# Values of four heads in one pass with tokens on partitions, and decay-level matmuls placed inside later projections

## The chip, the cores and the metric

The kernel runs on one core of one Trainium2 chip. The metric is the device time of one execution in microseconds, the median of several runs. A profile is one execution recorded by the hardware; its times are used below to work out costs.

## The reference, cut to what matters

One inference step of one layer that has two groups of heads. 512 prompt tokens and 64 sample tokens (8 sequences of 8) go through one input projection of 2048 inputs. Its outputs feed eight heads of sparse attention (a, 128 wide each), an indexer that picks the keys, and four heads of gated linear attention (b, keys 128 wide, values 256 wide).

```python
z = jnp.einsum('btd,de->bte', h, w_in)
qa, ka, va, ga, qi, ki, wi, qb, kb, vb, gb, ab = jnp.split(z, offs, axis=-1)
...
# sparse attention: scores against the picked keys, softmax, then the values va
# gated linear attention, in chunks:
cum = jnp.cumsum(at, axis=2)                       # log decays, summed along the chunk
o_inter = jnp.einsum('bhtk,bhkv->bhtv', qt * jnp.exp(cum), S)
att = jnp.einsum('bhtk,bhsk,bhtsk->bhts', qt, kt, decay)
o = o_inter + jnp.einsum('bhts,bhsv->bhtv', att, vt)
S_new = jnp.exp(last) * S + jnp.einsum('bhsk,bhsv->bhkv', kt * jnp.exp(last - cum), vt)
...
return einsum('bte,ed->btd', concatenate([a, bpart]), w_out)
```

The values `va` (1024 columns) and `vb` (1024 columns) are the part of the projection that the change concerns. New keys and values are outputs as well.

## The kernel before, in words

**Projection.** The input is kept transposed in SBUF, 16 pieces of 128 inputs by 576 tokens, each split into a high and a low part (`xh`, `xl`). `gemm(b)` (L207 on) computes one block of 128 output columns for all 576 tokens, with the columns on partitions: four weight pieces come by DMA (`wload`, L178), ScalarE casts the high part (L181), VectorE or GpSimd takes the low part (L183), and TensorE does three products for each of 16 input pieces in two halves of 288 tokens. That is 96 matmuls at L219 for a block. There are 65 such blocks or narrower ones in a fixed sequence: first block, indexer, then q, k, v and g of attention heads 0 to 7, then q, k and two value blocks of each gated head 0 to 3, then eight gates and the out-projection (L1133 to L1138, 512 columns moved against 128 stationary tokens or inputs).

**Values before.** A value block comes out with columns on partitions, though the attention needs tokens there. So `head_v` (L594 on) and the loop of the gated head (L982 on) write it to SBUF and turn it with five TensorE transposes (L601 and L607, L988 and L991).

**Accumulators.** PSUM holds two accumulators of two banks for `gemm` (`pg`), three single banks (`pm`) that everything else shares in turn, and one bank for the paged attention.

**Work beside the projections.** Generators are advanced between the weight pieces: `fill` advances the scoring of cached index keys (`first`, rate `RF`) and later the paged attention of the sample tokens (`us`, rates `R0`, `R1`); `pump` advances the selection of the top keys (`bg`), which runs mostly on VectorE during attention heads 0 to 3.

**A gated head before.** `log_decay(h)` makes the summed log decays `cum`: two matmuls into `ps_z` (L850), then ScalarE takes an absolute value, an exponential and a logarithm (L851, L853, L854), VectorE adds and scans (L855, L857). Seven levels follow (block sizes 64 to 1): GpSimd subtracts (L887, L888, tile `lv_d`), ScalarE takes the exponential (L889), VectorE multiplies with keys and queries (L890, L891), and TensorE does a run of small matmuls into `pl` for the first four levels and another for the rest (`run`, L252 and L255). `kD` (L958 to L961) is the key factor for the state; it is turned by TensorE. The recurrence over the four chunks and the sample states comes after the value blocks. `log_decay(h+1)` is called ahead of the recurrence of head h, and `cum` has two buffers.

**What sets the order.** Each engine runs its own list of instructions in the order in which a scheduler has placed them. The scheduler goes by the order of the code and by buffers coming free; weight loads and the tails of runs are given a higher priority. Within a list, an instruction that waits holds all that stand behind it.

Of the kernel before, what the change touches and what calls it, by code (L numbers as in the profile page):

```python
# [119 lines left out]
def build(tc, I, O):  # L120
# [4 lines left out]
    R0, R1, RF = 0.42, 0.8, 2  # L125
# [187 lines left out]
    spill_a = [dp.tile([P, TP], F32, name=f"sa{h}") for h in range(HA)]  # L313
    spill_o = [dp.tile([P, T], F32, name=f"so{h}") for h in range(HA)]
# [35 lines left out]
    rs2 = v2(rstd)  # L350
    sst2 = pa.tile([P, 5], F32, name="sst2")
# [3 lines left out]
    def token_scales():  # L355
        sst = pr.tile([P, 5], F32, name="sst")
        ve.memset(sst, 1.0)
        for i in range(5):
            r = P if i < 4 else TS
            xt = pr.tile([P, D], F32, name="xt", bufs=2)  # L360
            with tc.issue_after(wloads[3]):
                sy.dma_start(xt[:r], I["xp"][P * i : P * (i + 1)] if i < 4 else I["xs"])
            se.activation(xt[:r], xt[:r], AF.Square, accum_out=sst[:r, i : i + 1])
# [3 lines left out]
        for j in range(2):  # L367
            pst = mm1("ps_st")
            for i in (range(4), (4,))[j]:
                n = (P, TS)[j]  # L370
                dg = pr.tile([P, P], F32, name="dg", bufs=2)
                ve.tensor_scalar(out=dg[:, :n], in0=ident[:, :n], scalar1=sst[:, i : i + 1], scalar2=None, op0=ALU.mult)
# [220 lines left out]

    def head_v(h):  # L594
        ps = gemm(11 + 4 * h)
        vT = ev.tile([P, T], F32, name="ev_v", tag="e1", bufs=2)
        ve.tensor_tensor(out=v2(vT), in0=ps, in1=rs2, op=ALU.mult)
        sy.dma_start(O["vT"][h], vT)
        pt = mm1("pt")
        for i in range(4):  # L600
            pe.transpose(pt[:, P * i : P * (i + 1)], vT[:, P * i : P * (i + 1)], ident)  # L601
        vh = px["p"].tile([P, 512], F32R, name="vh")
        vl = px["p"].tile([P, 512], F32R, name="vl")
        se.copy(vh, pt)
        ve.tensor_tensor(out=vl, in0=pt, in1=vh.bitcast(F32), op=ALU.subtract)
        pt = mm1("pt")
        pe.transpose(pt[:, :P], vT[:, T - P : T], ident)  # L607
        se.copy(vaS[TS:, P * h : P * (h + 1)], pt[TS:, :P])
# [52 lines left out]
    def head(h, bg, n):  # L661
        if h > 1:
# [4 lines left out]
        elif h == 1:  # L667
            q, k = qk1
        else:
            q = head_q(0)  # L670
            pump(bg, n)
            k = head_k(0)
            pump(bg, n)
            qk1.append(head_q(1))
            qk1.append(head_k(1))
# [5 lines left out]
        if h > 0:  # L681
            Pi = head_scores(h, q, k)
        v = head_v(h)
        pump(bg, n)
        if h == 0:
            Pi = head_scores(h, q, k)
        g1 = head_g(h)
        pump(bg, min(n, 3))
# [105 lines left out]
    head(0, bg, 17)  # L794
    head(1, bg, 3)
    head(2, bg, 3)
    head(3, bg, 3)
# [46 lines left out]
    def log_decay(h):  # L844
# [11 lines left out]
        cum = gl.tile([P, T], F32, name="cum", bufs=2)  # L856
# [3 lines left out]
    cum_next = log_decay(0)  # L860
    for h in range(HB):
        cum = cum_next
        b0 = 41 + 4 * h
        ps = gemm(b0)
        qT = gl.tile([P, T], F32, name="qT")
# [3 lines left out]
        ve.tensor_tensor(out=v2(kT), in0=ps, in1=rs2, op=ALU.mult)  # L869
        cP = cum[:, :TP].rearrange("p (i t) -> p i t", t=P)  # L870
        cS = cum[:, TP:T].rearrange("p (i t) -> p i t", t=DT)

# [5 lines left out]
        for B in (64, 32, 0, 16, 8, 4, 2, 1):  # L878
# [57 lines left out]
            if B in (16, 1):  # L936
                run(*(m for level in reversed(mms) for m in level))
# [6 lines left out]
        for w in range(2):  # L944
# [3 lines left out]
            )  # L948

        eC = ev.tile([P, T], F32, name="ev_ec", tag="e0", bufs=2)  # L950
        se.activation(eC, cum, AF.Exp, scale=G)
        eL = gl.tile([P, 12], F32, name="eL", bufs=2)
        po_.tensor_copy(eL[:, 0:4].unsqueeze(2), eC[:, :TP].rearrange("p (i t) -> p i t", t=P)[:, :, P - 1 : P])
        po_.tensor_copy(eL[:, 4:12].unsqueeze(2), eC[:, TP:T].rearrange("p (i t) -> p i t", t=DT)[:, :, DT - 1 : DT])
        qE = gl.tile([P, T], F32, name="qE", tag="lv_q")
        ve.tensor_mul(qE, qT, eC)
        kD = gl.tile([P, T], F32, name="kD", tag="lv_d", bufs=4)
        po_.tensor_tensor(out=kD[:, :TP].rearrange("p (i t) -> p i t", t=P), in0=cP[:, :, P - 1 : P].to_broadcast([P, 4, P]), in1=cP, op=ALU.subtract)  # L958
        po_.tensor_tensor(out=kD[:, TP:T].rearrange("p (i t) -> p i t", t=DT), in0=cS[:, :, DT - 1 : DT].to_broadcast([P, NB, DT]), in1=cS, op=ALU.subtract)
# [3 lines left out]
        for i in range(4):
            pe.transpose(pt[:, P * i : P * (i + 1)], kD[:, P * i : P * (i + 1)], ident)
        kDt = gl.tile([P, 4, P], F32, name="kDt")
        se.copy(kDt, pt.rearrange("p (i d) -> p i d", i=4))
        pt = mm1("pt")
        pe.transpose(pt[:, :P], kD[:, T - P : T], ident)
        kDs = ev.tile([TS, P], F32, name="kDs", tag="e1", bufs=2)
        se.copy(kDs, pt[TS:, :P])  # L970
        ks = [gl.tile([96, P], F32R, name=f"ks{w}") for w in range(2)]
        for w in range(2):
            r = slice(32 * w, 32 * w + 32)
            lo_r, hi_r = ((32, 0), (0, 32))[w]
            se.copy(ks[w][hi_r : hi_r + 32], kDs[r])
            se.copy(ks[w][64:96], kDs[r])
            ve.tensor_tensor(out=ks[w][lo_r : lo_r + 32], in0=kDs[r], in1=ks[w][r].bitcast(F32), op=ALU.subtract)
        Qd = bass.AP(tensor=Qb.tensor, offset=Qb.offset, ap=[Qb.ap[0], [64, 4], [32 + DT, 2], [1, DT]])
        po_.tensor_copy(Qd, qE[:, TP:T].rearrange("p (m e t) -> p m e t", e=2, t=DT))

        vtok = gl.tile([P, 4, DV], F32, name="vtok")
        for half in range(2):  # L982
            ps = gemm(b0 + 2 + half)
            vT = ev.tile([P, T], F32, name="ev_v", tag="e1", bufs=2)
            ve.tensor_tensor(out=v2(vT), in0=ps, in1=rs2, op=ALU.mult)
            pt = mm1("pt")
            for i in range(4):
                pe.transpose(pt[:, P * i : P * (i + 1)], vT[:, P * i : P * (i + 1)], ident)  # L988
            se.copy(vtok[:, :, P * half : P * (half + 1)], pt.rearrange("p (i d) -> p i d", i=4))
            pt = mm1("pt")  # L990
            pe.transpose(pt[:, :P], vT[:, T - P : T], ident)  # L991
            se.copy(vS[:TS, P * half : P * (half + 1)], pt[TS:, :P])
# [6 lines left out]

        if h + 1 < HB:  # L1000
# [63 lines left out]
    for _ in us:  # L1064
        pass
# [202 lines left out]
```

## Time and profile before

| | us |
|---|---|
| median of 3 runs | 1247.18 (1246.3 to 1252.36) |
| the profiled execution | 1248.29 |
| its span, first to last instruction | 1246.5 |
| TensorE busy (98% of the span) | 1225.0 |
| VectorE busy (52%) | 651.1 |
| ScalarE busy (45%) | 558.2 |
| GpSimd busy (22%) | 269.9 |
| mean granted TensorE clock, share of full speed | 0.996 |

The profiled execution lies 1.1 us above the median of the runs and 1.8 us above its own span. A busy time adds up the recorded durations of an engine's instructions. Matmuls overlap in the records (one of 288 columns is recorded with some 300 ns, and the next starts sooner than that), so a price for TensorE is read from the distance of starts. The four gated heads take the stretch from 623 to 920 us, the gates come next, and the out-projection is last.

### The profile page before, as it was taken

The page shows a single profiled execution, that of the slowest core. Times are in us where ns is not written, and L with a number is a line of the kernel's source. Part 1 is how long each engine was busy: PE and PEld are TensorE (multiplying, and loading weights), DVE is VectorE, ACT ScalarE, POOL GpSimd, SP SyncE. Part 2 cuts the span into 40 slices and gives each one's busy share as a digit, 9 for nine tenths or more (in the row PEclk, how much of TensorE's full clock was granted, in tenths as well). Part 3 has the DMA queues.
Part 4 walks back from the last instruction along what each step waited for, and adds up shares of the span by engine and source line. Part 5 has one row for each costly group of instructions (what it writes and reads, how often), then busy time and mean ns, then how long its engine had stood idle before and what let it go on. Part 6 is the DMA issues. An engine that isn't in the chain of part 4 may idle for free.

```text
span 1246.5 us, 24845 instructions
## 1 busy us (share of the span) xinstructions
PE 1225.0 (98%) x9419; PEld 1119.2 (90%) x9419; DVE 651.1 (52%) x1330; ACT 558.2 (45%) x1072; POOL 269.9 (22%) x355
## 2 busy tenths in 40 slices
PE   9999999999999999999999999999999999999997
PEld 8899989999998979898988888888989998888896
DVE  6678899997543434342445444554445442323242
ACT  7966675353343423342344533635445432223233
POOL 0224663454511010100104121131120200102021
PEclk9999999999999999999999999999999999999998
DMA  9652233223726575664667576581414534334335
GB/s 314 219 157 88 70 95 95 87 83 99 254 90 241 193 243 181 219 209 161 229 201 238 191 264 209 202 264 60 152 62 155 179 99 136 102 101 123 89 113 171
DMA packets 117610, 200.58 MB, mean 161 GB/s; under 512 B 13922, under 2 KB 30579, under 8 KB 116787
## 3 DMA queue, kind: packets, MB, share of 16 engines
q1 hardware_dynamic: 116402, 197.55, 48.4%
q8 instruction: 74, 1.21, 0.4%
q10 hardware_dynamic: 1088, 1.45, 0.3%
q14 instruction: 46, 0.37, 0.1%
HBM read 180.06 MB, written 18.76 MB: 160 GB/s over the span
## 4 chain that ended last, share of the span: by engine, by line
PE 85%; DVE 5%; issue 4%; DMA 2%; ACT 2%; POOL 1%; SPq 1%; DVEq 0%; ACTq 0%; POOLq 0%
PE ps_g L219 50%; PE ps_g L227 6%; PE acc L1133 5%; PE acc L1135 5%; PE acc L1134 5%; PE pOs L255 2%; PE pS L255 1%; DVE wk L496 1%; PE acc L1137 1%; PE acc L1138 1%; PE pOs L252 1%; PE pS L252 1%; DVE top L493 1%; PE pt L649 1%; SPq L157 1%
## 5 line engine op out<-in xcount | busy, mean ns | idle before, releaser
L219 PE MATMUL ps_g<-xh,w_hi 128*128 128x288 f32 x1824 | 401.8, 299 | 1.1 <-ACT w_hi L198 0.6
L219 PE MATMUL ps_g<-xh,w_lo 128*128 128x288 f32 x1824 | 399.0, 298 | 0.0
L219 PE MATMUL ps_g<-xl,w_hi 128*128 128x288 f32 x1824 | 398.1, 297 | 0.0
L181 ACT CAST w_hi<-w_raw 128x512 fp32r<-128x512 f32 x316 | 194.8, 619 | 413.6 <-PE ps_g L219 237.2
L183 DVE TENSOR_TENSOR w_lo<-w_raw,w_hi 128x512 fp32r<-128x512 f32 x252 | 177.5, 708 | 305.3 <-ACT w_hi L181 301.9
L219 PEld LDWEIGHTS ps_g<-xh,w_hi 128*128 128x128 f32 x1824 | 295.7, 189 | 15.9 <-issue 11.7
L219 PEld LDWEIGHTS ps_g<-xh,w_lo 128*128 128x128 f32 x1824 | 295.9, 189 | 3.6 <-issue 2.1
L219 PEld LDWEIGHTS ps_g<-xl,w_hi 128*128 128x128 f32 x1824 | 296.3, 189 | 2.6 <-issue 1.3
L1134 PE MATMUL acc<-w_lo,mh 128*128 128x512 f32 (+1 forms) x320 | 110.7, 346 | 0.0
L1135 PE MATMUL acc<-w_hi,ml 128*128 128x512 f32 (+1 forms) x320 | 110.6, 346 | 0.0
L1133 PE MATMUL acc<-w_hi,mh 128*128 128x512 f32 (+1 forms) x320 | 110.3, 346 | 0.0
L183 POOL TENSOR_TENSOR w_lo<-w_raw,w_hi 128x512 fp32r<-128x512 f32 x64 | 87.4, 1367 | 74.4 <-ACT w_hi L181 60.2
L1153 POOL TENSOR_TENSOR y<-y,nfb 128x512 f32<-128x512 f32 (+3 forms) x25 | 27.7, 1123 | 190.3 <-ACT yjk L1152 190.3
L1134 PEld LDWEIGHTS acc<-w_lo,mh 128*128 128x128 f32 x320 | 60.5, 189 | 7.5
L1133 PEld LDWEIGHTS acc<-w_hi,mh 128*128 128x128 f32 x320 | 60.4, 189 | 7.5
L1135 PEld LDWEIGHTS acc<-w_hi,ml 128*128 128x128 f32 x320 | 60.4, 189 | 7.5
L887 POOL TENSOR_TENSOR lv_d<-cum 128x256 f32<-128x256 f32 (+1 forms) x28 | 20.8, 742 | 132.0 <-DVE cum L857 78.8
L571 POOL TENSOR_TENSOR ev_sw<-ev_sw,c_s 128x576 f32<-128x576 f32 x16 | 22.9, 1432 | 118.7 <-ACT ev_sw L568 118.5
L227 PE MATMUL ps_g<-xh,w_hi 128*128 128x448 f32 x128 | 47.2, 370 | 0.7 <-ACT w_hi L181 0.4
L227 PE MATMUL ps_g<-xh,w_lo 128*128 128x448 f32 x128 | 47.0, 368 | 0.3 <-DVE w_lo L183 0.3
L227 PE MATMUL ps_g<-xl,w_hi 128*128 128x448 f32 x128 | 47.0, 367 | 0.0
L421 DVE SCALAR_TENSOR_TENSOR sc<-rl,wtok,sc 128x256 f32<-128x256 f32 (+2 forms) x45 | 35.9, 831 | 4.3 <-ACT rl L416 4.0
(334 smaller groups left out, 1631.5 us busy)
## 6 DMA issues: line engine op xcount, KB each, us to landing
w_raw<-in_w SPq DMA_DIRECT2D x252, 256.0 KB, 3.1
kt<-in_ck SPq DMA_DIRECT2D x128, 256.0 KB, 5.2
vt<-in_cv SPq DMA_DIRECT2D x128, 256.0 KB, 5.2
w_raw<-in_wo SPq DMA_DIRECT2D x64, 256.0 KB, 2.8
xr<-in_xT SPq DMA_DIRECT2D x16, 288.0 KB, 4.6
xt<-in_xp SPq DMA_DIRECT2D x4, 1024.0 KB, 7.3
st<-in_state SPq DMA_DIRECT2D x8, 512.0 KB, 5.7
out_ss<-st SPq DMA_DIRECT2D x8, 512.0 KB, 3.8
```

The lines of the kernel that those rows point to most:

```text
L181: se.copy(hi, raw)
L183: lo_eng[0].tensor_tensor(out=lo, in0=raw, in1=hi.bitcast(F32), op=ALU.subtract)
L219: pe.matmul(ps[:, j, :HT], wt, xt[:, j * HT : (j + 1) * HT], start=(k == 0 and n == 0), stop=(k == NK - 1 and n == 2),)
L227: pe.matmul(ps[:, 0, :TQ], wt[:, c], xt[:, P:T], start=(k == 0 and n == 0), stop=(k == NK - 1 and n == 2))
L252: lead = first()
L255: f()
L421: ve.scalar_tensor_tensor(out=sc[i], in0=rl[:, :n], scalar=wcol, in1=sc[i], op0=ALU.mult, op1=ALU.add)
L571: po_.tensor_tensor(out=sw, in0=sw, in1=S128, op=ALU.mult)
L1133: pe.matmul(acc, mh[k][:, tsl], wh, start=(k == 0), stop=False)
L1134: pe.matmul(acc, mh[k][:, tsl], wl, start=False, stop=False)
L1135: pe.matmul(acc, ml[k][:, tsl], wh, start=False, stop=(k == NK - 1))
L1153: po_.tensor_tensor(out=yc, in0=yc, in1=nfb[:r, cs], op=ALU.mult)
```

## The change

Four things change.

1. The 16 value blocks become four calls of `vgroup(g)`, each for 512 value columns. Tokens are the stationary operand, 128 at a time, and 512 weight columns move. The 64 sample tokens sit beside their own low parts in one 128-wide tile `xs`, which GpSimd copies for each input piece. Four accumulators are the halves of two `pg` tiles; the fifth, `ps_v`, is a `pm` bank. ScalarE evacuates with the token scale, and the rows go to a DRAM tile `spill_v` (and to the output). `head_v` reads its 128 columns back, `recur` reads 256. The transposes of values go. Group 0 comes after the keys of attention head 1, group 1 in head 4, groups 2 and 3 in gated heads 0 and 1.
2. The gated head is cut into `project` (with `log_decay` at its start), `decays` (a generator that yields ahead of each run) and `recur`. The runs of `decays(h)` are called inside the projection that follows: in `vgroup` for heads 0 and 1, in the projections of head 3 for head 2, and in the first two gates for head 3.
3. `log_decay(h+1)` is called after `recur(h)`, `cum` has one buffer, and `kD` is made ahead of the levels.
4. Rates: `R1` 0.8 to 0.65, `RF` 2 to 1.1, and `pump` advances 10 and 4 steps in place of 17 and 3.

The diff, cut to its core:

```diff
+    def vgroup(g, step):
+        two = [pg.tile([P, 2, 512], F32, name="ps_g", tag="ps_g") for _ in range(2)]
+        accs = [two[0][:, 0], two[0][:, 1], two[1][:, 0], two[1][:, 1], mm1("ps_v")]
+        def mms(i, k):
+            wh, wl = w[k]
+            a, b = k == 0, k == NK - 1
+            if i == 4:
+                pe.matmul(accs[4], xs2[k], wh, start=a, stop=False)
+                pe.matmul(accs[4], xs2[k], wl, start=False, stop=b)
+            else:
+                c = slice(P * i, P * i + P)
+                pe.matmul(accs[i], xh[k][:, c], wh, start=a, stop=False)
+                pe.matmul(accs[i], xh[k][:, c], wl, start=False, stop=False)
+                pe.matmul(accs[i], xl[k][:, c], wh, start=False, stop=b)
+        w, xs2 = [], []
+        for k in range(NK):
+            w.append(wload(I["wv"][g, :, k : k + 1, :]))
+            xs = ev.tile([P, P], F32R, name="xs", tag="xs", bufs=4)
...
+            if k == 1:
+                for i in (0, 1, 4, 2, 3):
+                    for kk in (0, 1):
+                        mms(i, kk)
...
+            if k % 2:
+                fill()
+            if k % 4 == 3:
+                step(k // 4)
+        for i in range(4):
+            vt = ev.tile([P, 512], F32, name="v_tok", tag="e1", bufs=2)
+            se.activation(vt, accs[i], AF.Copy, scale=sst[:, i : i + 1])
+            sy.dma_start(spill_v[g][r], vt)
...
     def head_v(h):
-        ps = gemm(11 + 4 * h)
...
+        v32 = px["p"].tile([P, 4, P], F32, name="v32")
+        sy.dma_start(v32, spill_v[h // 4][:TP, P * (h % 4) : P * (h % 4) + P].rearrange("(i p) c -> p i c", p=P))
...
-        cum = gl.tile([P, T], F32, name="cum", bufs=2)
+        cum = gl.tile([P, T], F32, name="cum")
...
+    def project(h):
+        cum = log_decay(h) if h < 3 else None
...
+    def decays(h, qT, kT, cum):
+        cum = cum or log_decay(h)
...
             if B in (16, 1):
+                yield
                 run(*(m for level in reversed(mms) for m in level))
...
+    def recur(h, eL, qE, kDt, ks):
         vtok = gl.tile([P, 4, DV], F32, name="vtok")
-        for half in range(2):
-            ps = gemm(b0 + 2 + half)
...
+        sv = spill_v[2 + h // 2][:, DV * (h % 2) : DV * (h % 2) + DV]
+        sy.dma_start(vtok, sv[:TP].rearrange("(i p) c -> p i c", p=P))
...
-        if h + 1 < HB:
-            cum_next = log_decay(h + 1)
...
+    for h in range(HB):
+        if h < 3:
+            pj = project(h)
+            next(pj)
+            d = decays(h, *next(pj))
+        else:
+            d = decays(h, *qk3)
+        next(d)
+        if h < 2:
+            vgroup(2 + h, lambda q4: next(d) if q4 in (0, 2) else None)
+        elif h == 2:
+            pj = project(3)
+            next(pj)
+            next(d)
+            qk3 = next(pj)
+            next(d)
...
+        else:
+            mg, mg_s = pool("mixg", 1, side="right")
+            for i in range(2):
+                gate(i)
+                next(d)
+        recur(h, *kept[h])
```

TensorE's list before, where `log_decay(1)` stands: in the second value block of gated head 0. Names: `ev_v` is the value block being turned, `ps_z` the decay input, `ps_g` the projection that goes on.

```order
L252 MATMUL pOs<-vt,prT 32x512
L255 MATMUL pOs<-vt,prT 32x512 x7
L988 MATMUL pt<-c_ident,ev_v 128x128 x4
L991 MATMUL pt<-c_ident,ev_v 128x128
L850 MATMUL ps_z<-abS,wgS 128x288
L219 MATMUL ps_g<-xl,w_hi 128x288
```

The decay input of head 1 stands ahead of that head's own projections, which follow it with their 96 matmuls a block.

TensorE's list after, where `log_decay(1)` stands now: inside group 3, behind the last steps of `recur(0)` (`osb`, the output rows of head 0). The lines are those of the changed kernel: L896 is `ps_z`, L949 and L953 turn `kD`, L604 and L605 are the fifth accumulator of the group, `ob` and `pS` belong to the paged attention.

```order
L1110 MATMUL pt<-c_ident,osb 128x128 x4
L1113 MATMUL pt<-c_ident,osb 128x128
L896 MATMUL ps_z<-abS,wgS 128x288 x2
L823 MATMUL pt<-c_ident,ob 128x128 x4
L755 LDWEIGHTS selw
L755 MATMUL pS<-biasS,selw 128x512
L949 MATMUL pt<-c_ident,kD 128x128 x4
L953 MATMUL pt<-c_ident,kD 128x128
L604 MATMUL ps_v<-w_hi,xs 128x512
L605 MATMUL ps_v<-w_lo,xs 128x512
```

Between the decay input and the turning of `kD`, which is computed from it, four transposes and one matmul are left.

GpSimd's list before, for gated head 1. `lv_d` is a level's difference, `eL` and `Qb` small copies, `qz` a buffer of the paged attention.

```order
L887 TENSOR_TENSOR lv_d<-cum 128x288
L888 TENSOR_TENSOR lv_d<-cum 128x288
L953 COPY eL<-ev_ec 128x4
L954 COPY eL<-ev_ec 128x8
L979 COPY Qb<-qE 128x4x2x8
L698 MEMSET qz 128x512
L703 COPY qz<-qaS 128x4x8 x4
L958 TENSOR_TENSOR kD<-cum 128x512
L959 TENSOR_TENSOR kD<-cum 128x64
L961 TENSOR_TENSOR kD<-kT,kD 128x576
```

GpSimd's list after, for the same head.

```order
L944 TENSOR_TENSOR kD<-cum 128x64
L981 TENSOR_TENSOR lv_d<-cum 128x4x64
L982 TENSOR_TENSOR lv_d<-cum 128x4x64
L981 TENSOR_TENSOR lv_d<-cum 128x8x32
L982 TENSOR_TENSOR lv_d<-cum 128x8x32
L981 TENSOR_TENSOR lv_d<-cum 128x16x16
L982 TENSOR_TENSOR lv_d<-cum 128x16x16
L744 MEMSET qz 128x512
L938 COPY eL<-ev_ec 128x4
L939 COPY eL<-ev_ec 128x8
L965 COPY Qb<-qE 128x4x2x8
L946 TENSOR_TENSOR kD<-kT,kD 128x576
```

`kD` has moved from behind all levels to the front, but its last step, the multiplication with the keys, stands behind six differences of three levels and the small copies.

## Rows read from the trace of the kernel before

**Rows 1.** The page's busy times: us, share of the span, instructions.
```profile
PE 1225.0 (98%) x9419; PEld 1119.2 (90%) x9419; DVE 651.1 (52%) x1330; ACT 558.2 (45%) x1072; POOL 269.9 (22%) x355
```
**Rows 2.** TensorE's waits: us in total, times, longest us.
```profile
PE pl L252 <- DVE lv_d L891: 4.6, 2, 2.7
PE pq L466 <- ACT kcl L463: 1.6, 1, 1.6
...
PE pl L252 <- DVE lv_d L890: 1.4, 1, 1.4
```
**Rows 3.** TensorE's timeline, a gate block: start, us, then instructions and their count.
```profile
984.73 0.42 PE L219 MATMUL ps_g<-xh,w_hi 128*128 128x288 f32 x2
...
993.53 0.43 PE L219 MATMUL ps_g<-xh,w_hi 128*128 128x288 f32 x2
```
**Rows 4.** TensorE's timeline in the out-projection.
```profile
1120.01 0.39 PE L1133 MATMUL acc<-w_hi,mh 128*128 128x512 f32 x1
...
1121.37 0.39 PE L1133 MATMUL acc<-w_hi,mh 128*128 128x512 f32 x1
```
**Rows 5.** TensorE's timeline, the transposes of a value block of attention.
```profile
258.85 0.60 PE L601 MATMUL pt<-c_ident,ev_v 128*128 128x128 f32 x4
259.28 0.27 PE L607 MATMUL pt<-c_ident,ev_v 128*128 128x128 f32 x1
260.03 0.53 PE L219 MATMUL ps_g<-xh,w_hi 128*128 128x288 f32 x2 [0.48 <-DVE ga L614]
```
**Rows 6.** TensorE's timeline around the longest wait of a decay run.
```profile
908.08 0.18 PE L252 MATMUL pl<-lv_d 128*32 128x16 f32 x1 [2.69 <-DVE lv_d L891]
...
909.61 0.61 PE L219 MATMUL ps_g<-xh,w_hi 128*128 128x288 f32 x1
...
912.41 0.45 PE L219 MATMUL ps_g<-xh,w_hi 128*128 128x288 f32 x2
```
**Rows 7.** ScalarE's timeline, the log decay of gated head 0.
```profile
646.25 0.89 ACT L851 ACTIVATE ld_e<-ps_z,bgate 128x288 f32<-128x288 f32 x2 [1.24 <-PE ps_z L850]
647.16 1.28 ACT L853 ACT_TABLE_LOAD   x1
648.46 0.68 ACT L853 ACTIVATE ld_e<-ld_e 128x576 f32<-128x576 f32 x1
...
649.67 1.28 ACT L854 ACT_TABLE_LOAD   x1
650.96 0.69 ACT L854 ACTIVATE ld_e<-ld_e 128x576 f32<-128x576 f32 x1
```
**Rows 8.** VectorE's timeline, the same stretch.
```profile
652.54 1.36 DVE L857 TENSOR_TENSOR_SCAN cum<-reset,ld_m 128x576 f32<-128x576 bf16 x1
```
**Rows 9.** GpSimd's timeline, the first four levels of the same head.
```profile
654.05 0.62 POOL L887 TENSOR_TENSOR lv_d<-cum 128x256 f32<-128x256 f32 x1 [18.05 <-DVE cum L857]
...
655.20 1.15 POOL L887 TENSOR_TENSOR lv_d<-cum 128x256 f32<-128x256 f32 x1
...
659.50 0.61 POOL L888 TENSOR_TENSOR lv_d<-cum 128x256 f32<-128x256 f32 x1
660.06 0.38 POOL L953 COPY eL<-ev_ec 128x4 f32<-128x4 f32 x1
...
660.52 0.23 POOL L979 COPY Qb<-qE 128x64 f32<-128x64 f32 x1
```
**Rows 10.** GpSimd's groups by line: busy us, mean ns, idle before.
```profile
L1095 POOL TENSOR_TENSOR og<-og,mo 128x576 f32<-128x576 f32 x7 | 10.0, 1430 | 97.5 <-DMA ma<-sa 51.6 <-ACT og L1092 45.3 <-DMA mo<-so 0.6
...
L961 POOL TENSOR_TENSOR kD<-kT,kD 128x576 f32<-128x576 f32 x4 | 5.7, 1421 | 3.2 <-ACT kD L960 3.2
...
L958 POOL TENSOR_TENSOR kD<-cum 128x512 f32<-128x512 f32 x4 | 4.4, 1107 | 15.9 <-PE pl L255 15.9
...
L959 POOL TENSOR_TENSOR kD<-cum 128x64 f32<-128x64 f32 x4 | 1.6, 404 | 0.0
```
**Rows 11.** Busy time by stretch: from:to, width, then PE, PEld, DVE, ACT, POOL.
```profile
150.00:260.00 110.00, 106.54 (x785) 99.52 (x783) 105.58 (x248) 56.53 (x99) 54.89 (x62) 1.00 0.31 95
```

More of the change, by code (lines that the diff above doesn't have):

```diff
@@ L313, in build @@
     spill_a = [dp.tile([P, TP], F32, name=f"sa{h}") for h in range(HA)]
+    spill_v = [dp.tile([T, 512], F32, name=f"sv{g}") for g in range(4)]
     spill_o = [dp.tile([P, T], F32, name=f"so{h}") for h in range(HA)]
@@ L661, in head @@
     def head(h, bg, n):
[L662 removed]
+        if h == 1:
+            q, k = qk1
+        else:
             q = head_q(h)
@@ L666, in head @@
             pump(bg, n)
[L667 to L675, printed above, removed]
+        if h == 0:
+            for f in (head_q, head_k):
+                qk1.append(f(1))
+                pump(bg, n)
+            vgroup(0, lambda q4: pump(bg, 2))
             filler[0] = None
@@ L793, in build @@
     lo_eng[0] = po_
[L794 to L797, printed above, removed]
+    head(0, bg, 10)
+    head(1, bg, 4)
+    head(2, bg, 4)
+    head(3, bg, 4)
     lo_eng[0] = ve
@@ L855, in log_decay, with gate @@
         ve.tensor_tensor(out=mn, in0=mn, in1=e_, op=ALU.subtract)
-        cum = gl.tile([P, T], F32, name="cum", bufs=2)
+        cum = gl.tile([P, T], F32, name="cum")
         ve.tensor_tensor_scan(out=cum, data0=reset, data1=mn, initial=0.0, op0=ALU.mult, op1=ALU.add)
         return cum
-    cum_next = log_decay(0)
-    for h in range(HB):
-        cum = cum_next
+    og, kept = [], {}
+    def gate(i):
+        ps = gemm(57 + i)
+        g1 = mg.tile([P, T], F32, name=f"og{i}")
+        ve.tensor_tensor(out=v2(g1), in0=ps, in1=rs2, op=ALU.mult)
+        se.activation(g1, g1, AF.Silu)
+        o_t = ev.tile([P, T], F32, name="mo", tag="e0", bufs=2)
+        sy.dma_start(o_t, spill_o[i])
+        (po_ if i < 7 else ve).tensor_tensor(out=g1, in0=g1, in1=o_t, op=ALU.mult)
+        og.append(g1)
+    def project(h):
+        cum = log_decay(h) if h < 3 else None
         b0 = 41 + 4 * h
         ps = gemm(b0)
-        qT = gl.tile([P, T], F32, name="qT")
+        qT = gl.tile([P, T], F32, name="qT", bufs=2)
         ve.scalar_tensor_tensor(out=v2(qT), in0=ps, scalar=float(P ** -0.5), in1=rs2, op0=ALU.mult, op1=ALU.mult)
+        yield
         ps = gemm(b0 + 1)
@@ L963, in build @@
[L963 to L977, printed above, removed]
@@ L978, in build @@
-        Qd = bass.AP(tensor=Qb.tensor, offset=Qb.offset, ap=[Qb.ap[0], [64, 4], [32 + DT, 2], [1, DT]])
-        po_.tensor_copy(Qd, qE[:, TP:T].rearrange("p (m e t) -> p m e t", e=2, t=DT))
-        vtok = gl.tile([P, 4, DV], F32, name="vtok")
-        for half in range(2):
-            ps = gemm(b0 + 2 + half)
[L984 to L992, printed above, removed]
+        yield
@@ L1063, in build, with mixed @@
             sy.dma_start(spill_o[2 * h + half], o_t)
-    for _ in us:
-        pass
-    un_s.close()
+    for h in range(HB):
[14 more added lines that the diff above has]
+            next(d)
+            for _ in us:
+                pass
+            filler[0] = None
+            un_s.close()
+        else:
+            mg, mg_s = pool("mixg", 1, side="right")
[3 more added lines that the diff above has]
+        recur(h, *kept[h])
     gl_s.close()
-    mg, mg_s = pool("mixg", 1, side="right")
     mp, mp_s = pool("ms", 1)
     mh, ml, ms = [], [], []
-    def mixed(k, src, smp, pl, tags):
-        h = pl.tile([P, tags[2]], F32R, name="mh", tag=tags[0])
+    def mixed(k, src, smp, h, l):
         se.copy(h[:, :TP], src[:, :TP])
-        l = pl.tile([P, tags[2]], F32R, name="ml", tag=tags[1])
         ve.tensor_tensor(out=l[:, :TP], in0=src[:, :TP], in1=h[:, :TP].bitcast(F32), op=ALU.subtract)
@@ L1085, in mixed @@
         ms.append(s)
[L1087 removed]
     for i in range(8):
[L1089 to L1096 removed]
+        if i > 1:
+            gate(i)
         src = ev.tile([P, TP], F32, name="ma", tag="e1", bufs=2)
         sy.dma_start(src, spill_a[i])
[L1099 removed]
+        h, l = mp.tile([P, TP], F32R, name=f"mh{i}"), mp.tile([P, TP], F32R, name=f"ml{i}")
+        mixed(i, src, mixS[:, i, :], h, l)
     for i in range(8):
[L1101 removed]
+        h, l = xp.tile([P, T], F32R, name="mh", tag="xh"), xp.tile([P, T], F32R, name="ml", tag="xl")
+        mixed(8 + i, og[i], og[i][:, TP:T], h, l)
     banks = [0, None]
```

125 lines of the change are left out of this document (74 added, 51 removed).

## The prediction

> **What bounds the kernel now.** I read the page's busy times first: TensorE is recorded busy for 1225.0 of 1246.5 us, no other engine for more than 52% [rows 1]. The reader is to see a kernel whose time is the length of TensorE's list, plus its few waits. The second view is TensorE's waits: the largest are two kinds of wait of a decay run for VectorE's last multiplication of a level, 4.6 and 1.4 us, and one of 1.6 us for a cast of cached index keys [rows 2]. The third is the timeline, for the distance of starts. In a gate block the rows from 984.73 to 993.53 lie 66 matmuls apart: 8.80 / 66 = 0.1333 us for 288 columns [rows 3]. In the out-projection six matmuls of 512 columns take 1121.37 - 1120.01 = 1.36, or 0.2267 us each [rows 4]. Four transposes of a value block take 259.28 - 258.85 = 0.43, or 0.108 each [rows 5]. So two things decide: how many columns go through TensorE, and whether a new place appears where it has to wait.
>
> **The change, part by part.** Everything is summed against the profiled execution (1248.3 us); the median of the runs shown is 1.1 lower.
>
> *Values.* Sixteen blocks of 96 matmuls go: 1536 x 0.1333 = 204.8 us. Sixteen times five transposes go: 80 x 0.108 = 8.6 us. Each group needs 16 input pieces x (4 token tiles x 3 + 2 for the samples) = 224 matmuls of 512 columns, four groups 896: at 0.2267 that is 203.1 us. Their form (128 rows, 128 stationary columns, 512 moved) is that of rows 4, so I take that distance. The net is 203.1 - 204.8 - 8.6 = -10.3. A wait of 0.48 behind one block's transposes [rows 5] goes as well: **-10.8**. The value pass as such therefore saves little; it is the transposes that go. Bounds: -10.3, if that wait only moves, and -12, if the other blocks lose 0.1 each where TensorE changes from one form to another.
>
> *Waits of the decay runs.* The 4.6 + 1.4 = 6.0 us [rows 2] go, since a run now stands behind a stretch of 512-column matmuls. After the longest of them the projection runs at half its speed: 11 matmuls from 909.61 to 912.41 take 2.80 us [rows 6], against 11 x 0.1333 = 1.47; the clock was at its lower level, 1.2 GHz, after TensorE had stood still for 2.69 us. That is 1.3 more. Together **-7.3**.
>
> *Rates.* The index scoring is spread over a longer stretch, so its 1.6 us wait [rows 2] may go or stay. I take **-1.0**, between 0 and -1.6.
>
> *The new wait in gated head 1.* In the new list `log_decay(1)` stands behind the whole of `recur(0)`, inside value group 3, and the turning of `kD` follows with four transposes and one matmul of 512 columns between: 4 x 0.108 + 0.23 = 0.7 us of work [rows 4, 5]. `kD` depends on it. The chain, priced by head 0 in the trace: from the first absolute value at 646.25 through a table load of 1.28, an exponential of 0.68, another load of 1.28, a logarithm of 0.69 [rows 7] to the end of the scan, 652.54 + 1.36 = 653.90 [rows 8], is 7.65 us. Then GpSimd, in the order of its new list: the two subtractions of `kD`, 1.107 + 0.404 = 1.5 [rows 10]; six differences of three levels, of which eight took 660.11 - 654.05 = 6.06, so 6 x 0.76 = 4.5 [rows 9]; the small copies, 660.06 to 660.75, 0.7 [rows 9]; the multiplication, 1.4 [rows 10]. That is 8.1, in all 15.8, with 0.3 for the matmul itself 16.1 us. Less 0.7 of work: TensorE stands still for about **15.4**. Before, the same chain lay beside a head's own q and k blocks (2 x 96 x 0.1333 = 25.6 us) and cost nothing. Nothing covers it now: behind the waiting transposes stand the fifth accumulator (which needs a bank of the shared pool), the decay run and the rest of group 3, and the five buffers of weights are held. With the differences at 0.62 each [rows 9] the wait would be 14.5; with three at 1.15, 17. Bringing the clock back costs more than after the 2.69 us wait, since the decay run and the paged scores also fall in the slow stretch: 1.3 measured, up to 4, I take **2.0**. The output transposes of head 0 and the `ps_z` banks ahead of it: **0.5** (0 to 1.5).
>
> The Trainium skill, in "ScalarE: Activation LUTs", section "What ACT_TABLE_LOAD costs", counts a drain of about 1380 ns with each switch of the table set, 2.66 us in all. The trace disagrees: the load takes 1.28 and the exponential starts 0.02 us after its end [rows 7]. By the page the chain would be 2.8 us longer in each head where it shows, and the time some 8 us higher; I go by the rows.
>
> *The same chain in the other heads.* In head 0 the list has 60 matmuls of 512 columns and one paged step between `ps_z` and `kD`: 60 x 0.2267 = 13.6 and about 1.5, against 16.1: 1 us of waiting. In head 2 it is 86 matmuls of 288 columns (11.5) and about 1.3 of paged work after the second `ps_z`, against some 15.6: 3 us. In head 3 it is 123 matmuls (16.4), but ScalarE switches to the gates' function in between (a load of 1.28, [rows 7]) and GpSimd has a gate's product of 1.43 ahead [rows 10], so the chain is some 18: 1.5 us. Together **+5.5**, between 0 (ScalarE and GpSimd a little faster than in head 0) and 12.
>
> *Read-back of values.* A group's rows go to DRAM and come back before `head_v` and `recur` can use them. In head 0 of either kind a projection block of 12.8 us stands between, so I take **+1.0** for both, between 0 and 4. During the first group VectorE is the tight engine: it was busy for 105.58 of 110 us from 150 to 260 [rows 11], with the selection of the keys, which the scores of attention head 0 wait for. The new group needs less of VectorE than the blocks it replaces, so I count nothing more there.
>
> The gates, the out-projection and the attention scores keep their matmuls: 0.
>
> Sum: 1248.3 - 10.8 - 7.3 - 1.0 + 15.4 + 2.0 + 0.5 + 5.5 + 1.0 = 1253.6; less 1.1 for the median of the runs: **1252 us**.
>
> **The rivals.**
>
> *The chains are short and covered (1241 us, faster by about the bound).* With GpSimd at its fast durations (six differences at 0.62, [rows 9]) the wait in head 1 is 14.5, the clock costs 1.0, heads 0, 2 and 3 wait for nothing, the read-back is hidden, and the small waits of before all go: 1248.3 - 12.0 - 7.3 - 1.6 + 14.5 + 1.0 = 1242.9, less 1.1 gives 1242; every microsecond by which the subtractions of `kD` and its product are also faster than their means brings it lower, so 1241. For it: while TensorE stands still the other engines have little else to do and should run at their fast rows. Against it: the list leaves 0.7 us of cover, and two table loads, the scan and six differences on one engine cannot run side by side. Were the chain covered in head 1 as well, the time would be near 1225, but nothing in the list speaks for that.
>
> *Each head waits (1262 us, slower).* If in heads 0, 2 and 3 the casts of weights on ScalarE and the low parts on VectorE stand between the steps of the chain, as some do in head 0 of the trace (differences of 1.15 against 0.62, [rows 9]), the chain grows by 2 to 3 us, and since cover and chain are nearly equal there, all of it shows: 4 us each, 12 in place of 5.5, 17.4 in place of 15.4 in head 1, and half a microsecond of slow clock after each: 1252.4 + 6.5 + 2.0 + 1.5 = 1262. It decides from the point where the chain is longer than about 16 us in heads 0 and 2, which my own estimate is already at.
>
> *The runs still wait (1258 us).* The change would not do what it is said to do if the second run of a head (levels 8 to 1) again stands ahead of its last multiplication: in heads 2 and 3 it follows about 60 matmuls of 288 columns, 8 us, and four levels of two differences at 0.76 take 6 on GpSimd alone. Then the 6.0 come back: 1258.
>
> **How the numbers follow.** The forecast has a chance of 0.45 (its own range 1246 to 1258), the short chains 0.27, each head waiting 0.20, the runs still waiting 0.08. About 0.5%, 6.2 us, is what a measurement of this kernel can tell from no change, so faster is under 1240.9 and slower over 1253.4. Faster: two thirds of the short chains, 0.18, and 0.06 of the forecast's low end, 0.24. Slower: 0.25 of the last two rivals and 0.14 of the forecast, 0.39. The rest, 0.37, is no change that can be told. The range 1236 to 1264 reaches from the short chains with head 1 waiting 5 us less than there, to waits in all four heads, and leaves out 0.2.
>
> **What would show it.** Right: TensorE's longest wait, 13 to 17 us, at the transposes of `kD` for GpSimd, once, in the first third of value group 3, some 130 to 150 us after the gated heads begin, with a row of half-speed matmuls behind it; small waits at the same line in the other heads; the old waits for VectorE's level products gone; matmuls of 512 columns in the groups 0.227 apart; TensorE's recorded instructions otherwise as before. Wrong: no wait above 5 us at that line (then the time is near 1235); a distance in the groups other than 0.227, where each 0.01 is worth 9 us; or long waits for values read back, for the fifth accumulator's bank, or for the selection of keys at the scores of attention head 0.

## The result: 1256.5 us, 0.6% slower

The changed kernel takes 1256.51 us (median of 6 runs, 1255.76 to 1257.47); the kernel before, beside it, 1248.34 (6 runs). The ratio is 1.0063, 95% interval 1.0046 to 1.0080. The forecast was 1252 us, with a range of 1236 to 1264. The profiled execution took 1255.76, 7.5 us more than that of the kernel before.

### The profile page after: what moved, and what is told of

Read it like the earlier page. It is cut to its first block, busy times and chain, and to the rows that moved or that the text cites. A ratio compares the mean times of both kernels' runs of the same rounds, so it can differ in the third digit from the quotient of the medians.

```text
span 1254.0 us, 23627 instructions
## 1 busy us (share of the span) xinstructions
PE 1218.5 (97%) x8695; PEld 1075.0 (86%) x8699; DVE 663.5 (53%) x1322; ACT 567.6 (45%) x1073; POOL 311.7 (25%) x483
## 4 chain that ended last, share of the span: by engine, by line
PE 85%; DVE 4%; ACT 3%; DMA 2%; POOL 2%; issue 2%; SPq 1%; DVEq 0%; ACTq 0%; POOLq 0%
PE ps_g L219 34%; PE acc L1207 5%; PE acc L1205 5%; PE acc L1206 5%; PE ps_g L227 5%; PE ps_g L608 5%; PE ps_g L609 5%; PE ps_g L610 5%; PE pS L255 1%; PE pOs L255 1%; PE ps_v L604 1%; PE acc L1210 1%; PE acc L1209 1%; PE ps_v L605 1%; PE pS L252 1%
## 5 line engine op out<-in xcount | busy, mean ns | idle before, releaser
L219 PE MATMUL ps_g<-xh,w_hi 128*128 128x288 f32 x1312 | 288.2, 299 | 0.7 <-ACT w_hi L198 0.7
L219 PE MATMUL ps_g<-xl,w_hi 128*128 128x288 f32 x1312 | 288.0, 298 | 0.0
L219 PE MATMUL ps_g<-xh,w_lo 128*128 128x288 f32 x1312 | 285.1, 297 | 0.0
L219 PEld LDWEIGHTS ps_g<-xh,w_hi 128*128 128x128 f32 x1312 | 212.9, 189 | 10.1 <-issue 5.9
L219 PEld LDWEIGHTS ps_g<-xh,w_lo 128*128 128x128 f32 x1312 | 212.8, 189 | 1.5 <-issue 0.4
L219 PEld LDWEIGHTS ps_g<-xl,w_hi 128*128 128x128 f32 x1312 | 213.0, 189 | 1.2 <-issue 0.6
L608 PE MATMUL ps_g<-w_hi,xh 128*128 128x512 f32 x256 | 101.1, 395 | 0.0
L609 PE MATMUL ps_g<-w_lo,xh 128*128 128x512 f32 x256 | 100.0, 391 | 0.0
L610 PE MATMUL ps_g<-w_hi,xl 128*128 128x512 f32 x256 | 99.7, 390 | 0.0
L608 PEld LDWEIGHTS ps_g<-w_hi,xh 128*128 128x128 f32 x256 | 48.1, 188 | 14.0 <-issue 3.4
```

Of the source, the lines that this page charges most:

```text
L219: pe.matmul(ps[:, j, :HT], wt, xt[:, j * HT : (j + 1) * HT], start=(k == 0 and n == 0), stop=(k == NK - 1 and n == 2),)
L608: pe.matmul(accs[i], xh[k][:, c], wh, start=a, stop=False)
L609: pe.matmul(accs[i], xh[k][:, c], wl, start=False, stop=False)
L610: pe.matmul(accs[i], xl[k][:, c], wh, start=False, stop=b)
```

## The profile after

The page's busy times answer to [rows 1].

```profile
PE 1218.5 (97%) x8695; PEld 1075.0 (86%) x8699; DVE 663.5 (53%) x1322; ACT 567.6 (45%) x1073; POOL 311.7 (25%) x483
```

TensorE is busy for 6.5 us less, in a span that is 7.5 us longer: it has less to do and waits more. Its waits, where before stood [rows 2]:

```profile
PE pt L949 <- POOL kD L946: 15.1, 3, 9.0
PE pt L823 <- ACT ob L820: 5.2, 1, 5.2
...
PE pv L704 <- ACT th L701: 1.0, 1, 1.0
```

The decay runs (`pl`) and the index keys are gone from the list. In their place stands L949, the transposes of `kD`, three times, and L823, four transposes of the paged attention. TensorE's timeline shows that the 5.2 us and the longest of L949 are one pause, in gated head 1, inside value group 3 (start, us, instruction, idle before it):

```profile
767.50 0.40 PE L896 MATMUL ps_z<-abS,wgS 128*128 128x288 f32 x1 [0.18 <-ACT oT L1111]
773.05 1.12 PE L823 MATMUL pt<-c_ident,ob 128*128 128x128 f32 x4 [5.16 <-ACT ob L820]
783.21 1.12 PE L949 MATMUL pt<-c_ident,kD 128*128 128x128 f32 x4 [9.04 <-POOL kD L946]
...
785.19 0.63 PE L604 MATMUL ps_v<-w_hi,xs 128*128 128x512 f32 x1
785.62 0.63 PE L605 MATMUL ps_v<-w_lo,xs 128*128 128x512 f32 x1
786.05 0.46 PE L604 MATMUL ps_v<-w_hi,xs 128*128 128x512 f32 x1
786.35 0.40 PE L605 MATMUL ps_v<-w_lo,xs 128*128 128x512 f32 x1
786.58 0.39 PE L604 MATMUL ps_v<-w_hi,xs 128*128 128x512 f32 x1
...
798.66 0.39 PE L608 MATMUL ps_g<-w_hi,xh 128*128 128x512 f32 x1
...
799.79 0.39 PE L610 MATMUL ps_g<-w_hi,xl 128*128 128x512 f32 x1
...
901.32 0.66 PE L949 MATMUL pt<-c_ident,kD 128*128 128x128 f32 x4 [1.99 <-POOL kD L946]
...
977.32 1.11 PE L949 MATMUL pt<-c_ident,kD 128*128 128x128 f32 x4 [4.03 <-POOL kD L946]
...
980.73 0.44 PE L219 MATMUL ps_g<-xh,w_hi 128*128 128x288 f32 x2
```

Three readings. From the decay input to the turning of `kD` TensorE does four transposes (the one matmul that its list has there as well is not among the records) and stands still for 5.16 + 9.04 = 14.2 us. Behind the pause the 512-column matmuls start 785.62 - 785.19 = 0.43 apart, half speed, until 786.05, and 786.58 - 786.35 = 0.23 apart from 786.35 on; the granted clock was 0.50 of full speed, 1.2 GHz, from 769.1 to 786.2 us. Undisturbed ones keep the distance of [rows 4]: five from 798.66 to 799.79 make 0.226. Gated heads 2 and 3 wait for 1.99 and 4.03 us at the same line; head 0 does not.

The chain that the pause waits for, on ScalarE, VectorE and GpSimd, answers to [rows 7 to 10].

```profile
768.45 1.28 ACT L899 ACT_TABLE_LOAD   x1
769.75 0.68 ACT L899 ACTIVATE ld_e<-ld_e 128x576 f32<-128x576 f32 x1
770.45 1.28 ACT L900 ACT_TABLE_LOAD   x1
...
772.33 0.67 ACT L820 ACTIVATE ob<-pOs,mxs 128x512 f32<-128x512 f32 x1
```
```profile
773.25 1.36 DVE L903 TENSOR_TENSOR_SCAN cum<-reset,ld_m 128x576 f32<-128x576 bf16 x1
```
```profile
774.75 1.04 POOL L943 TENSOR_TENSOR kD<-cum 128x512 f32<-128x512 f32 x1 [60.24 <-DVE cum L903]
775.75 0.81 POOL L944 TENSOR_TENSOR kD<-cum 128x64 f32<-128x64 f32 x1
...
779.61 0.79 POOL L982 TENSOR_TENSOR lv_d<-cum 128x256 f32<-128x256 f32 x1
780.35 0.52 POOL L744 MEMSET qz<- 128x512 f32 x1
...
781.59 1.57 POOL L946 TENSOR_TENSOR kD<-kT,kD 128x576 f32<-128x576 f32 x1
```

From the decay input at 767.50 to the end of the product at 781.59 + 1.57 = 783.16 are 15.7 us; 16.1 were estimated. The paged output `ob`, for which TensorE waits first, stands in ScalarE's list behind the two table loads of the decay chain and has no wait of its own ahead of it.

## The experiments

Each was timed beside the kernel before on the same chip; the median of that was 1247.5 to 1248.6 us each time. Some waits are given 0.1 to 0.6 us longer in the expectations than the idle times in the rows (2.1 and 2.9 us in the kernel before, where the trace has 1.92 and 2.69); the measured figures are those of the rows.

**Log decay early.** `log_decay(h+1)` ahead of `recur(h)`:

```diff
-        cum = log_decay(h) if h < 3 else None
...
+    cum_next = log_decay(0)
     for h in range(HB):
...
+        if h + 1 < HB:
+            cum_next = log_decay(h + 1)
         recur(h, *kept[h])
```

Expected:

> The log decay of the next gated head is computed ahead of the recurrence of the present one, as in the kernel before; all else is the changed kernel (1256.5 us). Theory (the chain from the decay input to kD stops TensorE because nothing is left to cover it): the waits of 14.8, 2.2 and 4.2 us at the transposes of kD and the slow clock behind them (some 4.7 us in all) go, so about 1230 us, with no wait over 1 us at kD. Rival one (the wait only moves, to the decay runs as in the kernel before, 6 us and 1.3 of slow clock): about 1238 us with waits at pl. Rival two (the new value pass is what costs, through values read back or the fifth accumulator's bank): over 1250 us, with waits at vtok, ps_v or ps_g.

Measured: 1243.38 us, ratio 0.9966 (0.9954 to 0.9979), 13 us less than the changed kernel. The waits of TensorE:

```profile
PE pt L823 <- ACT ob L820: 3.4, 1, 3.4
PE pl L252 <- DVE lv_d L983: 2.8, 1, 2.8
PE pl L255 <- issue: 1.8, 1, 1.8
```

All waits for `kD` are gone, so the chain was the cause of those 20.2 us. But half of the expected gain was taken by other waits, 8.0 us, and by half speed behind them, as rival one had it in kind. ScalarE's row for `ob` names the cause of the first (what ended its idle time stands in brackets):

```profile
769.14 0.69 ACT L820 ACTIVATE ob<-pOs,mxs 128x512 f32<-128x512 f32 x1 [2.10 <-DMA so<-oT]
```

`ob` waits for a buffer of the pair `e0` that still holds the output rows `oT` of head 0, on their way to DRAM. For the wait of 2.8 us, in head 3, the trace shows no such row.

**`kD` product on VectorE, head 1 alone.**

```diff
-        po_.tensor_tensor(out=kD, in0=kT, in1=kD, op=ALU.mult)
+        (ve if h == 1 else po_).tensor_tensor(out=kD, in0=kT, in1=kD, op=ALU.mult)
```

Expected:

> The product of kD with the keys goes to VectorE, in gated head 1 alone; TensorE's list stays. Theory: in the changed kernel GpSimd ends that product at 783.2 because six differences and small copies stand ahead of it, while its other input is there at 777.3. VectorE should end it near 778.4, so the wait shrinks by 4.8 us: 1251.7 us, the wait at kD in head 1 near 4.3 in place of 9.0. Rival (GpSimd's list is not what ends last, the weights held or the levels' differences are): the wait reappears behind kD at the fifth accumulator or at the decay run, and the time stays at 1255 to 1257 us.

Measured: 1252.76 us, 3.7 less. The waits, and VectorE's row:

```profile
PE pt L949 <- POOL kD L946: 6.0, 2, 4.0
...
PE pt L949 <- DVE kD L946: 3.8, 1, 3.8
```
```profile
777.31 1.02 DVE L946 TENSOR_TENSOR kD<-kT,kD 128x576 f32<-128x576 f32 x1 [0.90 <-ACT kD L945]
```

The product ends at 778.33 in place of 783.16, and the wait falls from 9.0 to 3.8 us (expected 4.3). GpSimd's list (six differences and small copies ahead of the product) was 5 us of the pause. The trace has a later wait of about 1 us at the paged scores, which takes part of it back.

**Kept warm.** In head 1, ahead of the `kD` transposes:

```diff
+        for i in range(36 if h == 1 else 0):
+            pe.matmul(pt, xh[i % 16][:, :P], xh[i % 16][:, :512], start=True, stop=True)
```

Expected:

> 36 matmuls of 512 columns whose results are overwritten stand in the gap of gated head 1, between the paged transposes and those of kD. Theory (the half-speed matmuls behind the wait come from TensorE having stood still): the kD transposes and the eight matmuls behind them run 0.108 and 0.227 apart, the end of the gap stays where it was, and the time falls by 1 to 1.5 us to about 1255. Rival (they are slow because their inputs arrive late or through a busy PSUM bank): they stay at 0.43 apart and the time stays at 1256.5; if the extra matmuls run into the end of the gap, up to 1258.

Measured: 1253.76 us, 2.7 less. TensorE's timeline behind the gap:

```profile
784.25 0.60 PE L951 MATMUL pt<-c_ident,kD 128*128 128x128 f32 x4
784.68 0.27 PE L955 MATMUL pt<-c_ident,kD 128*128 128x128 f32 x1
...
785.02 0.39 PE L605 MATMUL ps_v<-w_lo,xs 128*128 128x512 f32 x1
785.26 0.40 PE L604 MATMUL ps_v<-w_hi,xs 128*128 128x512 f32 x1
```

The transposes run 0.108 apart and the group's matmuls 0.24, though the inputs are the same: the half speed came from standing still. The extra matmuls overran the gap's end by some 0.6 us, and the trace's last TensorE instruction is 1.6 us earlier. The timed gain is larger than that. The profiled execution lies 1.1 us above the median here and 0.8 below it for the changed kernel; what else is in it I leave open.

**Groups 0 and 1 alone.** The changed kernel with the gated heads of the kernel before (R1 0.8). Expected:

> Value groups 0 and 1 (the attention heads) stay as changed; the gated heads are those of the kernel before, with value blocks turned by transposes, log decay early and R1 at 0.8. It isolates half of the value pass. Theory: half of the value gain, 5 us, and the 1.6 us wait for the cast of index keys go from 1248.3, the waits of the decay runs (about 6) stay: about 1241 us. Rival one (a pass of 512 columns saves nothing, what the groups save is only the waits): about 1246. Rival two (the first group meets VectorE's key selection): waits at the scores or the softmax of head 0, and 1248 or more.

Measured: 1252.9 us, ratio 1.0029 (1.0008 to 1.0049). In the trace the gated heads begin at 616.5 us in place of 623.3, so the attention half gains its 6.8 us, as the theory had it. Then the old code of the gated heads takes 14 us longer than in the kernel before. The profiled execution (1255.37 us) lies 2.5 us above the median; by the median it is some 11.5. Its decay runs wait for 7.9 + 2.2 = 10.1 us, where they waited for 6.0 [rows 2]:

```profile
PE pl L252 <- DVE lv_d L937: 7.9, 2, 4.3
PE pl L252 <- ACT lv_d L935: 2.2, 1, 2.2
```

I had no reason for that until the pair `e0` was looked at. ScalarE's row ahead of the exponential of `cum` in head 1 shows it:

```profile
742.09 1.28 ACT L997 ACT_TABLE_LOAD   x1 [7.91 <-DMA so<-oT]
```

**`oT` in the levels' buffers**, with the log decay early, and alone:

```diff
-            o_t = ev.tile([P, T], F32, name="oT", tag="e0", bufs=2)
+            o_t = gl.tile([P, T], F32, name="oT", tag="lv_d", bufs=4)
```

Expected of both:

> The early log decay as in the first experiment (1243.4 us), and the output rows of a gated head (oT, on their way to DRAM) take a buffer of the levels' tag lv_d in place of the pair e0. Theory: what is left in the first experiment comes from that pair. In head 1 the paged output (ob) waits until oT has been written to DRAM, and TensorE's transposes of ob wait 3.4 us for it; in head 3 ev_ec waits for the same pair, GpSimd's copy of it holds the levels behind it, and the last decay run waits 2.9 us. Both waits and the slow clock behind them go: 8 to 11 us, so 1232 to 1236 us. Rival (the pair is not what ends last; ScalarE's list is): the waits for ob and at pl stay within 1 us of theirs and the time stays at 1242 to 1244.

> The same move of oT to the levels' buffers in the changed kernel, with the log decay left late. Theory: the paged transposes no longer wait, but they stand inside the wait for the chain to kD, whose end is set by cum and GpSimd; the waits in heads 1 to 3 keep their sum within 1 us and the time stays at 1255 to 1257. Rival (the pair of buffers sets the end of the chain, through ev_ec and the small copies that stand ahead of the product on GpSimd): the waits shrink by several us, 1250 or less.

Measured: 1237.8 us with the early log decay (ratio 0.9913, 0.9896 to 0.9930), 5.6 less than without the move and not the 8 to 11 expected. The waits for `ob` and the gap in `pl` went, others came:

```profile
PE pS L252 <- DMA kt<-in_ck: 2.3, 1, 2.3
PE pl L252 <- DVE lv_d L983: 2.3, 1, 2.3
PE pt L947 <- POOL kD L944: 1.8, 1, 1.8
```

GpSimd's differences of a level now stand still for the write of `oT`, 2.88 us in head 1 and 2.97 and 1.75 in head 3, since they share its buffers. How TensorE's wait for the paged keys (`kt`) hangs on that is not shown; all three waits are gone in the next version.

Alone the move brought 1255.32 us, about 1 us less, as the theory had it. The two halves of the pause in head 1 become one, of the same length:

```profile
PE pt L949 <- POOL kD L946: 20.9, 3, 14.8
```

So in the changed kernel the chain sets the pause, and the buffer pair only sets how it is divided.

**`oT` in the space of `vtok`**, which needs no new memory, with the early log decay; in the kernel before; and with groups 0 and 1 alone:

```diff
+        o2 = gl.tile([P, 2, T], F32, name="oT", tag="vtok")
         for half in range(2):
-            o_t = ev.tile([P, T], F32, name="oT", tag="e0", bufs=2)
+            o_t = o2[:, half]
```

Expected of the three:

> As the first experiment (early log decay, 1243.4 us), with the output rows oT in the space of vtok, which nothing needs at that time, so that neither the pair e0 nor the levels' buffers wait for their way to DRAM. Theory: in the version with oT in the levels' buffers (1237.8 us) two waits of 2.4 and 2.5 us in heads 1 and 3 followed from levels that waited for that DMA; with oT apart these go too, with some slow clock: 1231 to 1235 us, no wait over 1.5 us at kD, ob or pl. Rival (the waits come from GpSimd's and ScalarE's lists, not from the buffers): waits of 2 us or more stay at pl or kD and the time is 1237 to 1243.

> The kernel before (1248.3 us), with oT in the space of vtok and nothing else changed. Theory: the two longer waits of its decay runs, 2.1 and 2.9 us, come from ScalarE holding ev_ec back until oT has reached DRAM (it stood 5.6 us for that in head 1), so they and the slow clock behind them go, and the wait of 1.4 us in head 0, which no oT precedes, stays: 1241 to 1244 us. Rival (GpSimd's list of differences ends last, as I priced the chain): the waits stay within 1 us and the time at 1247 to 1249.

> As the experiment with the attention heads' groups alone (1252.9 us), with oT in the space of vtok. Theory: that kernel lost in its gated heads what it had gained before them (it was 6.8 us ahead when they began), by waits of 4.4 and 3.8 us at pl behind the same DMA and by gaps in TensorE's list; with oT apart the waits go and it ends 4 to 7 us below the kernel before with oT apart, at 1235 to 1242. Rival (the groups cost the gated heads time in another way, through the order of the list or its gaps): 1248 us or more.

The first took 1233.59 us, ratio 0.9880 (0.9864 to 0.9897), within the 1231 to 1235 expected. It is better than both kernels. Of its waits only one is over 1.1 us, at `pl`, where none over 1.5 was expected, and it has no releaser:

```profile
PE pl L255 <- issue: 2.4, 1, 2.4
```

The kernel before with `oT` apart took 1241.94 us, ratio 0.9951 (0.9935 to 0.9966), as expected. In the kernel before ScalarE stood still for `oT` ahead of `ev_ec`:

```profile
742.92 1.28 ACT L951 ACT_TABLE_LOAD   x1 [5.57 <-DMA so<-oT]
```

With `oT` apart, the waits at L891 of [rows 2] are gone and the one of head 0, which no `oT` precedes, stays:

```profile
PE pq L466 <- ACT kcl L463: 1.6, 1, 1.6
PE pt L649 <- DVE p L638: 1.4, 1, 1.4
PE pl L252 <- DVE lv_d L890: 1.4, 1, 1.4
```

This is also the fair comparison for the change. With `oT` apart in both, the kernel before takes 1241.94 us and the changed kernel with the early log decay 1233.59, 8.3 less.

Groups 0 and 1 alone with `oT` apart took 1244.93 us: 8 us less than without, but 3 more than the kernel before with the same edit, so neither answer holds whole. In the profiled executions its gated heads begin 5 us earlier (619.5 against 624.5) and then lose 11.5; this execution (1247.97 us) lies 3.0 above its median, and by the medians they lose some 8. Of the 11.5 the trace shows gaps without a releaser, the longest in a run of small matmuls, and half speed behind it:

```profile
676.60 1.34 PE L255 MATMUL pl<-lv_d 128*32 128x16 f32 x133
680.30 0.29 PE L255 MATMUL pl<-lv_d 128*32 128x16 f32 x2 [2.36 <-issue]
...
681.16 0.68 PE L219 MATMUL ps_g<-xl,w_hi 128*128 128x288 f32 x2
```

Such gaps (2.4, 0.9 and 0.4 us), 2.8 us of half speed and 0.8 more at the first run make 7.3 of the 11.5 us. The rest stays open.

**The run cut in two.** In the best version, at the levels 8 to 1:

```diff
-            if B in (16, 1):
-                yield
+            if B in (16, 4, 1):
+                if B != 4:
+                    yield
                 run(*(m for level in reversed(mms) for m in level))
```

Expected, of this and of the best version once more beside it:

> As the version with early log decay and oT in the space of vtok (1233.6 us), with the second decay run (138 small matmuls one after the other) cut in two, so that two runs of 68 and 70 stand some 40 to 80 projection matmuls apart. Theory: the one long gap left, 2.4 us in which TensorE waited for nothing that the profile shows, 126 matmuls into that run of head 3, comes from small matmuls being executed faster than TensorE's list is supplied; shorter runs don't get there. The gap and the 2.5 us of half speed behind it go: 1228 to 1230 us. Rival (the gap sits at a place of the list, not at the length of a run): a gap of 1 to 3 us stays somewhere among the runs and the time is 1232 to 1235.

> The version with early log decay and oT in the space of vtok once more, beside the split run on the same chip: 1232.5 to 1234.5 us, with the gap of 2.4 us at the same matmul if it belongs to the program, elsewhere or absent if it does not.

Measured: 1231.61 us, ratio 0.9870 (0.9852 to 0.9889), and 1233.03 for the other, 0.9879 (0.9861 to 0.9897). The repeated program has the gap at the same matmul as the first time, behind 129 of the run (the expectation says 126):

```profile
943.38 1.26 PE L255 MATMUL pl<-lv_d 128*32 128x16 f32 x124
947.29 0.30 PE L255 MATMUL pl<-lv_d 128*32 128x16 f32 x11 [2.65 <-issue]
...
948.55 0.42 PE L219 MATMUL ps_g<-xh,w_lo 128*128 128x288 f32 x2
948.82 0.60 PE L219 MATMUL ps_g<-xl,w_hi 128*128 128x288 f32 x2
949.21 0.69 PE L219 MATMUL ps_g<-xh,w_hi 128*128 128x288 f32 x2
```

With shorter runs no such gap is in the waits:

```profile
PE pv L704 <- ACT th L701: 1.2, 2, 0.9
...
PE pO L1065 <- DVE Sst L1076: 1.0, 1, 1.0
```

That it vanished with shorter runs agrees with the theory but does not show it: the kernel before, with and without `oT` apart, and the changed kernel have runs of the same length and no such gap. The time fell by 1.4 us, less than the 4 expected, and the two intervals overlap, so the gain itself is not settled. What TensorE lacks in such a gap, and why the same length of run does not always bring it, is open.

## Why the prediction was right, and where its sizes were off

The forecast, a wait of TensorE for the chain to `kD` that eats what the value pass and the old waits gave, is what happened. By its own terms, in the profiled executions:

| term | predicted | measured | from |
|---|---|---|---|
| values, old softmax and index waits, attention half | -5.4 - 1.0 | -7.3 | start of the gated heads, 616.0 against 623.3 |
| values, gated half | -5.4 | -4.3 | not measured apart; taken from the attention half, below |
| waits of the decay runs and their slow clock | -7.3 | -7.3 | no wait at `pl` is left |
| pause in head 1 | +15.4 | +14.2 | 5.16 + 9.04 |
| slots ahead of it | +0.5 | +0.6 | waits at L1113 (0.4) and L896 (0.2) |
| waits in heads 0, 2, 3 | +1 + 3 + 1.5 | 0 + 2.0 + 4.0 | timeline |
| slow clock behind the waits | +2.0 | +4.7 | below |
| values read back | +1.0 | 0 | no wait for them on TensorE |

The right column makes +6.6, where the executions differ by 7.5; 0.9 us stay without a place. The start of the gated heads is itself uncertain by a microsecond: the first q block begins at 111.6 against 110.8 us, and at 111.6 too in the kernel before with `oT` apart, whose code up to there is that of the kernel before.

That the forecast came so near is in part luck. The predicted terms add up to +5.3. The pause was put 1.2 us too high and the read-back 1.0, which hides part of the slow clock, put 2.7 too low. And of the 4.5 us by which the forecast was low, the terms make 2.2. Another 1.1 was taken off for the median of three runs; over six runs the median of the kernel before is 1248.34, where its profiled execution lies. The rest is 0.5 of rounding and the 0.8 by which the changed kernel's profiled execution lies below its median.

**Right.** The pause's place in the list, its length (chain 15.7 against 16.1) and what releases its end; it lies 152 to 167 us after the gated heads begin, not 130 to 150, and its first 5.2 us are a wait at the paged transposes, not at those of `kD`. That most matmuls of the groups start 0.227 us apart, and that the value pass as such saves little.

**Mis-sized: the value pass.** The term was -10.8, or -5.4 a half. Added up from each start to the next in the two traces up to the gated heads, the blocks and transposes that went took 107.5 us and the 448 matmuls of the two groups take 103.3. That is 4.3 us for this half: the groups' mean distance is 0.2305, changes between kinds of matmul included. Of the other 3.0 us of this stage TensorE's waits make 1.5, and four softmax transposes that now come later 0.4; 1.1 has no place. Twice 4.3 is near the 8.3 us by which the two kernels with `oT` apart differ, though these differ in other waits too.

**Mis-sized: the slow clock.** The sum had 2.0 us, behind head 1 alone. It fell behind all three pauses. After 783.21 five transposes and six matmuls of 512 columns take 786.58 - 783.21 = 3.37 against 5 x 0.108 + 6 x 0.227 = 1.90: 1.5 us. In head 3, 977.32 to 980.73 holds five transposes, a decay run (1.1 at full speed) and one projection matmul, 3.4 against 1.8: 1.6. In head 2 the granted clock was 0.50 from 902.2 to 905.7 us, which costs about the same. That is 4.7 in all, 2.7 more than the term.

**Mis-sized: head 3.** The wait was 4.0, not 1.5: ScalarE put a third table load and the gate's function between exponential and logarithm (expected), a cast of weights stood ahead of the decay's first load, and the product waited behind a gate's product of 1.57 us. From the second decay input at 956.6 to the product's end at 977.26 the chain is 20.7 us, where some 18 were estimated.

**A cause read wrongly.** The step on the old waits took [rows 2] at its word, VectorE's last multiplication, and said that they go because a run now stands behind a longer stretch. The experiment on the kernel before shows what was behind them: ScalarE held the exponential of `cum` until `oT` had reached DRAM, because both use the pair `e0`; with `oT` apart 1.9 and 2.7 us of waiting went. In the changed kernel no engine's wait ends with that write: with the log decay late, ScalarE comes to `ev_ec` at 774.64 us, 7 us after it has written `oT`. The hold came up as soon as the log decay was early: 3.4 us in head 1, where the row of `ob` names it, and 2.8 in head 3, where only the experiment with `oT` apart shows it. So the gain that a repair of the pause promised by the ledger, 26 us, came to 13, and the rest only with `oT` moved: 1256.5, 1243.4, 1233.6.

The table loads at 768.45 and 770.45 us take 1.28 us each in the changed kernel too, and the exponential starts 0.02 us behind the first. The Trainium skill, in "ScalarE: Activation LUTs", section "What ACT_TABLE_LOAD costs", counts a drain of about 1380 ns with each. The trace does not agree: the pause came out shorter than estimated without a drain, not longer.

## What to carry to other kernels

When a producer's call moves, write down for each consumer what still stands between the two in the waiting engine's list, and price the whole chain in the order of the other engines' lists. Ask of each wait not only which engine came last but what that engine had waited for: a buffer of a shared pair that drains to DRAM looks like a slow engine. And expect that a removed wait shows the next one; count a repair's gain only after looking for it. Give the kernel before the same repair where it has the same fault, or the repair's gain is booked to the change.

## What the runs showed of the hardware that was not expected

TensorE paused for 1.5 to 2.7 us within long runs of 16-column matmuls (about 9 ns from start to start) in four versions, with no releaser in the trace, in one program at the same matmul in two profiles; the run cut in two had no such pause. And after the pause of 2.65 us shown above the projection ran at full speed first (0.27 for two matmuls) and fell to half speed (0.48) only 1.6 us after its end; the granted clock was 0.50 from 948.9 to 952.3 us. In the other profile of the same program, after 2.44 us at the same matmul, the first projection matmuls already ran at half speed and went on so for some 6 us (947.5 to 953.9 us). So one and the same pause has had two prices, and the price does not always lie right behind it.
